# Filter spectra and forward transform in three products of split parts, and modulation pieces of 128 columns, in a two-layer Hyena and attention block

## Chip, cores and metric

The kernel runs on one core of a Trainium2 chip. The metric is the device time of one execution in microseconds (us); lower is better. The time before is 1493.73 us, the median of 3 runs (1493.24 to 1494.67). Differences of about 0.2% (3 us) are what a measurement of this kernel can tell from none.

## The reference, cut to what matters

Layer 0 is a bidirectional Hyena mixer over 512 latent tokens and, with the same weights, over 256 context tokens; layer 1 is grouped-query attention. In front of each layer stands a modulation of the normalised tokens, and behind it a gate, both from a condition vector (one for latents, one for context):

```
sh, sc, gt = jnp.split(sc_lat @ ada_w[i] + ada_b[i], 3, axis=-1)      # ada_w[i]: 1024 x 3072
h_lat = rms_norm(x_lat, norm_g[i]) * (1.0 + sc[:, None]) + sh[:, None]
...
proj = h @ w_in                                                       # 1024 -> 4 * 2048
x0, x1, v = jnp.split(short_conv(proj[..., :3 * E_HY], conv_w, conv_b), 3, axis=-1)
u = x1 * v
k = hyena_filter(L, ...)                                              # from a small MLP, per channel
U = jnp.fft.rfft(u, n=2 * L, axis=1); K = jnp.fft.rfft(k, n=2 * L, axis=0)
y = jnp.fft.irfft(U * K[None], n=2 * L, axis=1)[:, :L]
y = ((y + u * d_skip) * x0) * silu(z)                                 # then @ w_out
```

All in float32. The change touches the computation of K from k, of U from u, and of the modulation rows `sc_lat @ ada_w + ada_b`.

## The kernel before

Matrix products that need float32 accuracy are made in one of two ways. A float32 matmul is given to TensorE as it is, which the trace shows as two matmul records for one. A product in split parts (`mm3`, L69 to L72) first splits each operand into a high part, rounded to 12 bits (type fp32r), and the rest; three fp32r matmuls (high by high, high by low, low by high) then add up in one PSUM tile. The high part of a tile is a cast on ScalarE, the low part a subtraction, for the weights mostly on GpSimd (`load_w`, L121 and L122: `stg` is the loaded tile, `whi` and `wlo` are its parts, two buffers of each).

Layer 0 runs in eight rounds g = 0 to 7, each for 256 of the 2048 channels, that is two tiles of 128 (j = 0, 1). A round has eight in-projections of 128 rows: `x1` and `v` of tile a, `x1` and `v` of tile b (both in `u_stage`), `z` of a (`z_stage`), `x0` of a (`x0_stage`), `z` of b, `x0` of b. One in-projection is eight steps (`in_step`, L453) of six fp32r matmuls, three of 512 columns for latents (tiles plx, plv, plz) and three of 256 for context (pcx, pcv, pcz). Between two steps is a slot, in which another piece of work can be issued to PE. The order within an engine is the order in which the program emits its instructions; a hand-written table `steps` (L673) and a list for each in-projection say what goes into which slot:

- `kdft(g, set)` (L408): spectra of the filter for four sets m, p, 0 (letters o/O) and c. The small letter emits the sums F = a + b and F = a - b on GpSimd (L424 and L425, tile `F`); the capital letter emits the matmuls `ks` with the constant `kmat` (L436: two PSUM tiles of 512 columns, each two matmuls of 256 columns), ScalarE's copy `ko` (L439), and VectorE's two sums `kt` (L442).
- `knorm` (n, N), `y_stage` of the round before (y, Y; matmuls `pq`, L603).
- a: one entry of the list `todo`, the modulation. Before, a piece has 256 columns of `ada_w` (tile `adw`, 1 MB by one DMA) and makes two entries. The first, `ada_rows` (L174 to L182), is 8 float32 matmuls `adar` of 256 columns that use 32 columns of the array each, in four groups that run side by side, and ScalarE's copy `adr`. The second, `ada_end` (L184), turns the sum over the four groups into columns by two matmuls `adap` (L189), or, for the pieces that belong to a gate, into rows by one matmul of 256 columns (L197), with a DMA of the bias in front and one or two DMAs to `g_scr` behind. There are 16 pieces. In rounds 1 to 7 the table has two letters a among `u_stage` and the `z` of tile a, and the `x0` of tile b carries two more, one behind its second step and one behind its last.
- `spectra(g, jt)` (L562): in the `x0` of tile a (jt = 0) and the `z` of tile b (jt = 1), three calls of `fwd` (L535: matmuls `pu`, two of 256 columns with `kfwd` as the stationary operand and `ut` moving), and VectorE's products with the filter spectra: `times` (L547), the sums (L571) and `combine` (L556, L557).
- The `x0` of tile b carries nothing of `spectra`, but the six lag tiles `pk` of the next round's filter (two matmuls each, L375 and L376, and VectorE's multiplication by the decay `dec`, L378, which comes by DMA into two buffers).

`ut`, the transposed u, is made by PE transposes (`turned`, L526 to L531) and one copy of ScalarE. All of ks, pu, pk, pq, pn, ut, adar and adap take their PSUM tile from one pool of four buffers in turn (`axt`): a matmul that takes a buffer waits until its reader of four tiles before is done.

Of the kernel before, what the change touches and what calls it, by code (L numbers as in the profile page):

```python
# [11 lines left out]
F32 = mybir.dt.float32  # L12
F32R = mybir.dt.float32r
# [6 lines left out]
P = 128  # L20
# [32 lines left out]
def hybrid_kernel(ctx: ExitStack, tc: tile.TileContext, x, c, ctxt, c_ctx, norm_g, ada_w, ada_b,  # L53
                  hy_w_in, hy_conv_w, hy_conv_b, fw1, fb1, fw2, fb2, fw3, fb3, fw4, freq, hy_d,
                  hy_w_out, at_w_in, at_q_g, at_k_g, at_w_out,
                  k_f, k_i, k_k, k_z, k_dec, k_rope, out, dbg=None):
# [25 lines left out]
    ones = gp.tile([P, P], F32, tag="ones", name="ones")  # L82
# [85 lines left out]
    def ada_load(l, o0):  # L168

        t = hp.tile([P, KD, 256], F32, tag="adw", name=f"adw_{l}_{o0}")  # L170
        nc.sync.dma_start(t, ada_w[l][:, o0:o0 + 256].rearrange("(k p) o -> p k o", p=P))
        return t

    def ada_rows(t, nm):  # L174

        pt = axt(f"adar{nm}")
        for k in range(KD):
            q = k % 4 * 32
            TE.matmul(pt[q:q + 32, 0:256], silp[:, k, :], t[:, k, :], start=k < 4, stop=k >= 4)
        r = hp.tile([P, 256], F32, tag="adr", name=f"adr{nm}")  # L180
        S.copy(r, pt[:, 0:256])
        return r  # L182

    def ada_end(l, o0, r, nm):  # L184

        pt = axt(f"adap{nm}")
        if o0 < 2 * DM:
            for j in range(2):
                TE.matmul(pt[:, 2 * j:2 * j + 2], r[:, j * P:(j + 1) * P], sel, start=True, stop=True)  # L189
            c_ = o0 // P  # L190
            V.tensor_tensor(ada[l].rearrange("p (s c) -> p c s", s=2)[:, c_:c_ + 2, :],
                            pt[:, 0:4].rearrange("p (j s) -> p j s", j=2),
                            vb[:, 32 + l * 24 + c_:32 + l * 24 + c_ + 2].unsqueeze(2).broadcast_to([P, 2, 2]), ALU.add)
# [1114 lines left out]
```

## Time and profile before

| | us |
|---|---|
| median of 3 runs | 1493.73 |
| the profiled execution | 1493.93 |
| its span, first to last instruction | 1492.1 |
| TensorE (PE) busy | 1465.7 (98%) |
| VectorE (DVE) busy | 1070.2 (72%) |
| ScalarE (ACT) busy | 516.8 (35%) |
| GpSimd (POOL) busy | 408.5 (27%) |

The granted clock of TensorE is 0.997 of full speed over the span. The rounds of layer 0 stand between about 50 and 812 us of the trace; a round takes some 95 us. A matmul's busy time overlaps that of its neighbours; what a group of matmuls takes of PE is read from the starts of the matmuls around it. Rows of the timeline give the start, the duration, the engine, the line, the operation, output and inputs, the shape, how many instructions were drawn together, and in brackets the idle time in front and what ended it.

### The profile page before, as it was taken

Reading aid. Unit: us, or ns where it says so; the run is one execution under the profiler, and the core shown is the slowest. Engines: PE = TensorE matmul, PEld = TensorE weight load, DVE = VectorE, ACT = ScalarE, POOL = GpSimd, SP = SyncE. Lnnn points to the kernel's source line nnn. Section 1 sums busy time; section 2 is a strip of 40 time slices with the busy share of each in tenths; the row PEclk is TensorE's granted clock in tenths of the full one; section 3 lists DMA queues with packets and bytes.
Section 4 is the critical chain, followed back from the end, with each engine's and each line's share of the span. In section 5 each row is a group of like instructions: output and inputs, shape, how many; then the busy total and the mean of one; then the engine's idle time right before and its main releaser. Section 6 shows DMA issues by size and latency. Waiting matters only on the chain. (4 is left out here: it accounts for less than half of the span.)

```text
span 1492.1 us, 22543 instructions
## 1 busy us (share of the span) xinstructions
PE 1465.7 (98%) x8791; PEld 1255.9 (84%) x8791; DVE 1070.2 (72%) x1864; ACT 516.8 (35%) x1009; POOL 408.5 (27%) x384
## 2 busy tenths in 40 slices
PE   8999999999999999999999999999999999999998
PEld 1788887888878888888888878799998998998987
DVE  5768759578495784966849454656787878878886
ACT  3432221222213222122132243534445444445442
POOL 3431523325234243342444351211110000000005
PEclk9999999999999999999999999999999999999999
DMA  8622323323233133231322776255222312312111
GB/s 297 190 86 78 97 59 92 99 81 89 78 92 93 54 109 92 71 113 50 96 93 85 280 253 198 74 155 173 93 92 72 99 43 71 98 44 71 57 62 66
DMA packets 158402, 156.66 MB, mean 105 GB/s; under 512 B 6683, under 2 KB 138354, under 8 KB 157784
## 3 DMA queue, kind: packets, MB, share of 16 engines
q1 hardware_dynamic: 154296, 134.77, 29.0%
q0 software_dynamic: 3856, 19.93, 3.8%
q8 instruction: 69, 1.13, 0.3%
q10 hardware_dynamic: 144, 0.52, 0.1%
q14 instruction: 37, 0.30, 0.1%
HBM read 137.36 MB, written 17.84 MB: 104 GB/s over the span
## 5 line engine op out<-in xcount | busy, mean ns | idle before, releaser
L122 POOL TENSOR_TENSOR wlo<-stg,whi 128x1024 fp32r<-128x1024 f32 x64 | 159.2, 2488 | 331.9 <-ACT whi L121 331.9
L121 ACT CAST whi<-stg 128x1024 fp32r<-128x1024 f32 x99 | 103.9, 1049 | 320.1 <-issue 135.2
L873 POOL TENSOR_TENSOR r2q<-s2q,mhalf 128x2 f32<-128x2 f32 x32 | 23.4, 731 | 343.6 <-DVE s2q L871 343.6
L455 PE MATMUL plx<-h_hi,whi 128*128 128x512 f32 x248 | 107.5, 433 | 0.0
L1102 ACT ACTIVATE E<-sc,st 128x768 f32<-128x768 f32 x64 | 57.7, 902 | 126.8 <-DVE st L1100 114.0
L459 PE MATMUL plx<-h_hi,wlo 128*128 128x512 f32 x248 | 98.0, 395 | 0.0
L456 PE MATMUL plx<-h_lo,whi 128*128 128x512 f32 x248 | 97.5, 393 | 0.0
L1099 DVE TENSOR_REDUCE st<-sc 128x1 f32<-128x768 f32 x64 | 61.0, 953 | 17.5 <-PE sc L72 17.2
L460 PE MATMUL pcx<-hc_hi,wlo 128*128 128x256 f32 x248 | 69.5, 280 | 0.0
L457 PE MATMUL pcx<-hc_hi,whi 128*128 128x256 f32 x248 | 69.5, 280 | 0.0
L458 PE MATMUL pcx<-hc_lo,whi 128*128 128x256 f32 x248 | 69.4, 280 | 0.0
L1119 DVE TENSOR_TENSOR ptl<-et,pth 128x768 fp32r<-128x768 f32 x64 | 61.1, 954 | 5.3 <-ACT pth L1118 4.0
L752 DVE TENSOR_TENSOR yl<-yf,yh 128x768 fp32r<-128x768 f32 x26 | 26.0, 1002 | 52.2 <-ACT yh L751 46.9
L1118 ACT CAST pth<-et 128x768 fp32r<-128x768 f32 x64 | 51.1, 799 | 31.2 <-PE et L1114 31.0
L455 PEld LDWEIGHTS plx<-h_hi,whi 128*128 128x128 f32 x248 | 46.7, 188 | 16.3 <-issue 7.5
L455 PE MATMUL plz<-h_hi,whi 128*128 128x512 f32 x128 | 58.0, 453 | 0.0
L457 PEld LDWEIGHTS pcx<-hc_hi,whi 128*128 128x128 f32 x248 | 46.5, 188 | 11.1
L458 PEld LDWEIGHTS pcx<-hc_lo,whi 128*128 128x128 f32 x248 | 46.5, 187 | 10.8
L72 PE MATMUL po<-pth,kvt 128*128 128x256 f32 x192 | 54.1, 282 | 0.0
L71 PE MATMUL po<-ptl,kvt 128*128 128x256 f32 x192 | 54.0, 281 | 0.0
L70 PE MATMUL po<-pth,kvt 128*128 128x256 f32 x192 | 53.9, 281 | 0.0
L611 ACT ACTIVATE qs<-pq,rn 128x256 f32<-128x256 f32 (+1 forms) x32 | 13.5, 420 | 116.3 <-PE pq L603 60.6
(751 smaller groups left out, 4873.4 us busy)
## 6 DMA issues: line engine op xcount, KB each, us to landing
stg<-in_hy_w_in_dram SPq DMA_DIRECT2D x64, 512.0 KB
stg<-in_at_w_in_dram SPq DMA_DIRECT2D x40, 512.0 KB
adw<-in_ada_w_dram SPq DMA_DIRECT2D x16, 1024.0 KB
yf<-y_scr POOLq DMA_DIRECT2D x32, 384.0 KB, 5.4
ad<-in_ada_w_dram SPq DMA_DIRECT2D x16, 512.0 KB
stg<-in_hy_w_out_dram SPq DMA_DIRECT2D x16, 512.0 KB
stg<-in_at_w_out_dram SPq DMA_DIRECT2D x16, 512.0 KB
dec<-in_k_dec_dram SPq DMA_DIRECT2D x48, 128.0 KB
```

The source lines that it names most:

```text
L72: TE.matmul(ps, ll, rh, start=False, stop=last)
L121: S.copy(hi, st)
L122: (lo_eng or lo_default[0]).tensor_tensor(lo, st, f(hi), ALU.subtract)
L455: TE.matmul(pl, hi[:, k, :], h_hi[:, k, :], start=fi, stop=False)
L456: TE.matmul(pl, hi[:, k, :], h_lo[:, k, :], start=False, stop=False)
L457: TE.matmul(pc[:, 0:LC], hi[:, k, :], hc_hi[:, k, :], start=fi, stop=False)
L458: TE.matmul(pc[:, 0:LC], hi[:, k, :], hc_lo[:, k, :], start=False, stop=False)
L459: TE.matmul(pl, lo[:, k, :], h_hi[:, k, :], start=False, stop=la)
L460: TE.matmul(pc[:, 0:LC], lo[:, k, :], hc_hi[:, k, :], start=False, stop=la)
L1099: V.tensor_reduce(st[:, 0:1], sc[:, 0:T], AX.X, ALU.max)
L1102: S.activation(E, sc[:, 0:T], AF.Exp, bias=st[:, 1:2], scale=scale, accum_out=st[:, 2:3])
L1119: V.tensor_tensor(pts[n // 2][1][:, :, o:o + P], tv, f(dh), ALU.subtract)
```

## The change

1. `kdft` and `fwd` use `mm3`. The constants come from the host as high and low parts (`k_khi`, `k_klo`, `k_fhi`, `k_flo`: four DMAs on GpSimd's queue rather than two). Behind each F stand a cast `Fh` on ScalarE and a subtraction `Fl` on GpSimd; F itself now has 1 buffer rather than 4, `Fh` and `Fl` have 2 each. `ut` becomes `uth` (ScalarE's copy) and `utl` (VectorE, PSUM tile minus `uth`), 1 buffer each rather than 2.
2. The modulation pieces have 128 columns: 32 pieces, 512 KB each. One entry of `todo` (`item`) now issues the 8 matmuls `adar` of a piece and the one matmul `adap` of the piece before. All pieces are summed to columns (L187, 128x2) with VectorE's bias sum (L188). The gate's rows are made once behind the last round: `gate_rows`, three PE transposes, one copy and three DMAs.
3. The first row of the table for rounds 1 to 7 gets one more a, in the `x1` of tile a behind the sixth step.

```diff
-        pt = axt(f"adap{nm}")
-        if o0 < 2 * DM:
-            for j in range(2):
-                TE.matmul(pt[:, 2 * j:2 * j + 2], r[:, j * P:(j + 1) * P], sel, start=True, stop=True)
...
-        TE.matmul(pt[0:2, 0:256], sel, r, start=True, stop=True)
...
+        pt, c_ = axt(f"adap{nm}"), o0 // P
+        TE.matmul(pt[:, 0:2], r, sel, start=True, stop=True)
+        V.tensor_scalar(ada[l].rearrange("p (s c) -> p c s", s=2)[:, c_, :], pt[:, 0:2],
+                        vb[:, 32 + l * 24 + c_:32 + l * 24 + c_ + 1], None, ALU.add)
...
-            F = kg.tile([P, 512], F32, tag="F", name=f"F{g}{nm}{par}", bufs=4)
+            F = kg.tile([P, 512], F32, tag="F", name=f"F{g}{nm}{par}")
...
-            banks.append(F)
+            Fh = kg.tile([P, 512], F32R, tag="Fh", name=f"Fh{g}{nm}{par}", bufs=2)
+            Fl = kg.tile([P, 512], F32R, tag="Fl", name=f"Fl{g}{nm}{par}", bufs=2)
+            S.copy(Fh, F)
+            G.tensor_tensor(Fl, F, f(Fh), ALU.subtract)
+            banks.append((Fh, Fl))
...
-                    TE.matmul(pt[:, r_], kmat[:, mset, par, cs, :], banks[par][:, r_], start=True, stop=True)
+                    Fh, Fl = banks[par]
+                    mm3(pt[:, r_], kmat[0][:, mset, par, cs, :], kmat[1][:, mset, par, cs, :],
+                        Fh[:, r_], Fl[:, r_], True, True)
...
-            S.copy(ut[:, b:b + n, j * P:(j + 1) * P], pv)
+            dh = uth[:, b:b + n, j * P:(j + 1) * P]
+            S.copy(dh, pv)
+            V.tensor_tensor(utl[:, b:b + n, j * P:(j + 1) * P], pv, f(dh), ALU.subtract)
...
-            TE.matmul(pu[:, cs * 256:(cs + 1) * 256], kfwd[:, cs, c_], ut[:, 2 * b + cs, :], start=True, stop=True)
+            mm3(pu[:, cs * 256:(cs + 1) * 256], kfwd[0][:, cs, c_], kfwd[1][:, cs, c_],
+                uth[:, 2 * b + cs, :], utl[:, 2 * b + cs, :], True, True)
...
-        for n in range(len(pieces)):
-            todo.extend([lambda n=n: products(n), lambda n=n: end(n)])
+        def item(n):
+            if n < len(pieces):
+                l, o0 = pieces[n]
+                r = ada_rows(adw.pop(0), f"_{l}_{o0}")
+            if n:
+                ada_end(*pieces[n - 1], box.pop(), f"_{pieces[n - 1][0]}_{pieces[n - 1][1]}")
...
-    steps = (("m - y - - - - -", "- - Mp - Y - - -", "- - Po - - a - -", "- n Oc - N - - -", "- - C - a - - -"),
+    steps = (("m - y - - a - -", "- - Mp - Y - - -", "- - Po - - a - -", "- n Oc - N - - -", "- - C - a - - -"),
```

What this moves on the engines is shown at three places. A row gives the line, the operation, output and inputs, the shape, and in brackets the semaphores that it waits for.

First, PE at the second slot of the `x0` of tile b in round 1 (plx0_3, pcx0_3 are its PSUM tiles). Before, the slot holds the eight products `adar` alone:

```order
L459 MATMUL plx0_3_1985<-h_hi_69,wlo16_1981 128x512
L460 MATMUL pcx0_3_1986<-hc_hi_71,wlo16_1981 128x256
L179 MATMUL adar_0_2816_1999<-adw_0_2816_1579,silp_128 32x256 [waits DMAHW6_49,PE_49]
L179 MATMUL adar_0_2816_1999<-adw_0_2816_1579,silp_128 32x256 x7
L455 MATMUL plx0_3_1985<-h_hi_69,whi16_1980 128x512
L456 MATMUL plx0_3_1985<-h_lo_70,whi16_1980 128x512
```

Now it is followed by the sum of the piece before, which waits for VectorE:

```order
L465 MATMUL plx0_3_2224<-h_hi_69,wlo16_2220 128x512
L466 MATMUL pcx0_3_2225<-hc_hi_71,wlo16_2220 128x256
L179 MATMUL adar_0_2944_2238<-adw_0_2944_1970,silp_128 32x128 [waits DMAHW7_49,PE_49]
L179 MATMUL adar_0_2944_2238<-adw_0_2944_1970,silp_128 32x128 x7
L187 MATMUL adap_0_2816_2249<-sel_131,adr_0_2816_1965 128x2 [waits DVE_49,PE_49]
L461 MATMUL plx0_3_2224<-h_hi_69,whi16_2219 128x512
L462 MATMUL plx0_3_2224<-h_lo_70,whi16_2219 128x512
```

The products became half as wide, and a second PSUM tile is taken in this slot: `adap` needs the buffer of the transform pu of (g, b = 0, jt = 1), which VectorE reads in its product ab·11a (· stands for the round).

Second, PE at the end of the same in-projection. Before, the last lag tile `pk2_5` is followed by the sum of the piece whose products stood in the second slot:

```order
L460 MATMUL pcx0_3_1986<-hc_hi_71,wlo16_1981 128x256
L375 MATMUL pk2_5_2091<-w4h2_2021,h3_199 128x512 [waits DVE_49]
L376 MATMUL pk2_5_2091<-w4l2_2022,h3_199 128x512
L197 MATMUL adap_0_2816_2095<-adr_0_2816_2008,sel_131 2x256 [waits DVE_49]
L455 MATMUL plx1_4_2116<-h_hi_69,whi17_2111 128x512
L456 MATMUL plx1_4_2116<-h_lo_70,whi17_2111 128x512
```

Now a whole item stands there:

```order
L466 MATMUL pcx0_3_2225<-hc_hi_71,wlo16_2220 128x256
L375 MATMUL pk2_5_2333<-w4h2_2263,h3_199 128x512 [waits DVE_49]
L376 MATMUL pk2_5_2333<-w4l2_2264,h3_199 128x512
L179 MATMUL adar_1_0_2337<-adw_1_0_2252,silp_128 32x128 [waits DMAHW3_49,DVE_49]
L179 MATMUL adar_1_0_2337<-adw_1_0_2252,silp_128 32x128 x7
L187 MATMUL adap_0_2944_2348<-sel_131,adr_0_2944_2247 128x2 [waits DVE_49]
L461 MATMUL plx1_4_2367<-h_hi_69,whi17_2362 128x512
```

It waits for VectorE's multiplications of two lag tiles, `pk2_2` (the products) and `pk2_3` (the sum), where one wait for `pk2_2` stood.

Third, POOL at the start of round 3 (F3m0 and F3m1 are the two tiles F of set m, wlo26 the low part of a weight tile). Before:

```order
L424 TENSOR_TENSOR F3m0_2930<-kfl3_2834 128x256 [waits DVE_49]
L425 TENSOR_TENSOR F3m0_2930<-kfl3_2834 128x256
L424 TENSOR_TENSOR F3m1_2933<-kfl3_2834 128x256
L425 TENSOR_TENSOR F3m1_2933<-kfl3_2834 128x256
L424 TENSOR_TENSOR F3p0_3049<-kfl3_2834 128x256
L425 TENSOR_TENSOR F3p0_3049<-kfl3_2834 128x256
L122 TENSOR_TENSOR wlo26_3013<-stg26_3011,whi26_3012 128x1024 [waits DMAHW5_49,PE_49,Activation_49]
```

Now:

```order
L424 TENSOR_TENSOR F3m0_3320<-kfl3_3212 128x256 [waits DVE_49]
L425 TENSOR_TENSOR F3m0_3320<-kfl3_3212 128x256
L122 TENSOR_TENSOR wlo26_3427<-stg26_3425,whi26_3426 128x1024 [waits DMAHW7_49,PE_49,Activation_49]
L431 TENSOR_TENSOR Fl3m0_3324<-F3m0_3320,Fh3m0_3323 128x512 [waits Activation_49]
L424 TENSOR_TENSOR F3m1_3327<-kfl3_3212 128x256 [waits DVE_49,Pool_49]
L425 TENSOR_TENSOR F3m1_3327<-kfl3_3212 128x256
L431 TENSOR_TENSOR Fl3m1_3331<-F3m1_3327,Fh3m1_3330 128x512 [waits Activation_49]
```

Each F is followed by its `Fl`, which waits for ScalarE's cast `Fh`; the second F waits for the first `Fl`, since F has one buffer, and `wlo26` moved ahead of the first `Fl`.

## Rows read from the trace of the kernel before

**Rows 1.** Busy time by stretch: us, then busy (x count) of each engine, clock.

```profile
296.80:308.20 11.40, 11.40 (x68) 10.14 (x67) 4.09 (x7) 3.68 (x7) 3.70 (x2) 1.00 0.27 77
319.50:330.70 11.20, 11.20 (x74) 9.15 (x73) 11.17 (x15) 2.19 (x4) 2.38 (x1) 1.00 0.18 52
```

**Rows 2.** Timeline of PE: a plain step's border, and one forward transform.

```profile
320.32 0.28 PE L460 MATMUL pcz<-hc_hi,wlo 128*128 128x256 f32 x1
...
320.67 0.39 PE L456 MATMUL plz<-h_lo,whi 128*128 128x512 f32 x1
...
321.37 0.28 PE L460 MATMUL pcz<-hc_hi,wlo 128*128 128x256 f32 x1
321.49 1.02 PE L541 MATMUL pu<-ut,kfwd 128*128 128x256 f32 x4
...
322.58 0.40 PE L456 MATMUL plz<-h_lo,whi 128*128 128x512 f32 x1
```

**Rows 3.** Timeline of PE: one set of filter spectra (round 3, set m).

```profile
354.47 0.28 PE L460 MATMUL pcv<-hc_hi,wlo 128*128 128x256 f32 x1
354.59 1.89 PE L436 MATMUL ks3m<-F3m,kmat 128*128 128x256 f32 x8
...
356.55 0.39 PE L456 MATMUL plv<-h_lo,whi 128*128 128x512 f32 x1
```

**Rows 4.** Timeline of PE: products of a piece, round 2, second slot of x0 b.

```profile
327.49 0.28 PE L460 MATMUL pcx<-hc_hi,wlo 128*128 128x256 f32 x1
327.70 1.07 PE L179 MATMUL adar<-adw,silp 128*32 128x256 f32 x16
...
329.04 0.39 PE L456 MATMUL plx<-h_lo,whi 128*128 128x512 f32 x1
```

**Rows 5.** Timeline of PE: sum of a gate piece behind the last round.

```profile
811.70 0.28 PE L460 MATMUL pcx<-hc_hi,wlo 128*128 128x256 f32 x1
811.91 0.59 PE L197 MATMUL adap<-adr,sel 128*2 128x256 f32 x2
...
812.77 0.39 PE L71 MATMUL po<-wlo,yhl 128*128 128x512 f32 x1
```

**Rows 6.** Timeline of DVE: products of round 2, and a lag multiplication behind.

```profile
308.62 1.23 DVE L547 TENSOR_TENSOR ab200b<-pu,kt2m 128x1024 f32<-128x1024 f32 x1 [0.68 <-PE pu L541]
...
326.61 2.58 DVE L556 TENSOR_TENSOR Y<-ab210a 128x256 f32<-128x256 f32 x1
329.11 0.41 DVE L557 TENSOR_TENSOR Y<-ab210a 128x256 f32<-128x256 f32 x1
329.44 1.21 DVE L547 TENSOR_TENSOR ab211a<-pu,kt2p 128x1024 f32<-128x1024 f32 x1
...
339.01 1.29 DVE L378 TENSOR_TENSOR kfl<-pk,dec 128x512 f32<-128x512 f32 x2 [2.04 <-DMA dec<-in_k_dec_dram]
```

**Rows 7.** Timeline of PE: waits in the x0 of tile b, round 2.

```profile
331.93 0.47 PE L375 MATMUL pk<-w4h,h 128*128 128x512 f32 x1 [0.38 <-DVE ab211b L547]
...
339.76 0.61 PE L189 MATMUL adap<-sel,adr 128*128 128x2 f32 x4 [0.98 <-DVE kfl L378]
340.23 0.49 PE L455 MATMUL plx<-h_hi,whi 128*128 128x512 f32 x1
```

**Rows 8.** Timeline of DVE: last operation of the last convolution, round 7.

```profile
815.18 0.47 DVE L505 SCALAR_TENSOR_TENSOR cvx<-pcx,vb,cvx 128x255 f32<-128x255 f32 x1
```

**Rows 9.** Timeline of POOL and of ACT, rounds 2 and 3.

```profile
340.64 0.74 POOL L424 TENSOR_TENSOR F3m<-kfl 128x256 f32<-128x256 f32 x1 [11.74 <-DVE kfl L382]
...
355.96 1.46 POOL L424 TENSOR_TENSOR F<-kfl 128x256 f32<-128x256 f32 x1
...
394.57 1.31 POOL L365 TENSOR_TENSOR w4l<-w4s,w4h 128x512 fp32r<-128x512 f32 x1 [4.51 <-ACT w4h L364]
...
393.88 0.62 ACT L364 CAST w4h<-w4s 128x512 fp32r<-128x512 f32 x1 [4.41 <-DMA w4s<-in_hy_fw_dram]
```

**Rows 10.** Chain that ended last, out-projection: start us, us, what.

```profile
884.54 3.79 POOL xr L771 x3
```

More of the change, by code (lines that the diff above doesn't have):

```diff
@@ L81, in hybrid_kernel @@
     make_identity(nc, ident)
-    ones = gp.tile([P, P], F32, tag="ones", name="ones")
+    ones = gp.tile([P, 1], F32, tag="ones", name="ones")
     G.memset(ones, 1.0)
@@ L300, in hybrid_kernel @@
     halves = [ytile(f"x{i}") for i in range(6)]
-    ux = [hp.tile([P, 6, 256], F32, tag="ut", name=f"xut{i}", bufs=2) for i in range(2)]
+    ux = [f(hp.tile([P, 6, 256], F32R, tag=t, name=f"x{t}")) for t in ("uth", "utl")]
     halves += [u_[:, 2 * i:2 * i + 2, :].rearrange("p a b -> p (a b)") for u_ in ux for i in range(3)]
@@ L522, in u_stage @@
         if j == 0:
-            uts[g] = hp.tile([P, 6, 256], F32, tag="ut", name=f"ut{g}", bufs=2)
-        ut = uts[g]
+            uts[g] = [hp.tile([P, 6, 256], F32R, tag=t, name=f"{t}{g}") for t in ("uth", "utl")]
+        uth, utl = uts[g]
         def turned(b, n):
@@ L623, in ada_items @@
         box = []
-        def products(n):
-            l, o0 = pieces[n]
-            if n == 0:
-                adw.append(ada_load(l, o0))
-            box.append(ada_rows(adw.pop(0), f"_{l}_{o0}"))
+        def item(n):
[4 more added lines that the diff above has]
+                ada_end(*pieces[n - 1], box.pop(), f"_{pieces[n - 1][0]}_{pieces[n - 1][1]}")
+            if n < len(pieces):
+                box.append(r)
             if n + 1 < len(pieces):
                 adw.append(ada_load(*pieces[n + 1]))
-        def end(n):
-            l, o0 = pieces[n]
-            ada_end(l, o0, box.pop(0), f"_{l}_{o0}")
-        for n in range(len(pieces)):
-            todo.extend([lambda n=n: products(n), lambda n=n: end(n)])
-    ada_items([(l, o) for l, a, b in ((0, 2048, 3072), (1, 0, 3072)) for o in range(a, b, 256)])
+        for n in range(len(pieces) + 1):
+            todo.append(lambda n=n: item(n))
+    pieces = [(l, o) for l, a, b in ((0, 2048, 3072), (1, 0, 3072)) for o in range(a, b, P)]
+    ada_items(pieces)
     def ada_next():
@@ L661, in hybrid_kernel @@
     begin((16, 32), filter_items(0))
[L662 to L665 removed]
+    adw.append(ada_load(*pieces[0]))
+    kmat = []
+    for i, src in enumerate((k_khi, k_klo)):
+        kmat.append(k0.tile([P, 2, 2, 2, P], F32R, tag=f"kmat{i}", name=f"kmat{i}"))
+        with after(hc_done[2]):
+            G.dma_start(kmat[i], src.rearrange("p (a b c d) -> p a b c d", a=2, b=2, c=2))
     kinv = kg.tile([P, 2, 2, P], F32, tag="kinv", name="kinv")
     nc.sync.dma_start(kinv, k_i.rearrange("p (a b c) -> p a b c", a=2, b=2))
[L668 to L669 removed]
+    kfwd = []
+    for i, src in enumerate((k_fhi, k_flo)):
+        t = k0.tile([P, 2, 256], F32R, tag=f"kfwd{i}", name=f"kfwd{i}")
+        with after(hc_done[2]):
+            G.dma_start(t, src.rearrange("p (a b) -> p a b", a=2))
+        kfwd.append(t)
     none = lambda: None
[L673 removed]
+    steps = (("m - y - - a - -", "- - Mp - Y - - -", "- - Po - - a - -", "- n Oc - N - - -", "- - C - a - - -"),
              ("- - - - - - - -", "- - - - - - - -", "nm - - - Mp - - -", "N Po - - - Oc - -", "- a - C - a - -"))
@@ L700, in hybrid_kernel @@
     make_gsc(1)
+    gate_rows()
     p0.close()
@@ L733, in early_tiles @@
             return yf, t[:, 0, 0:T], t[:, 1, 0:T]
-        t = hp.tile([P, 6, 256], F32R, tag="ut", name=f"yhl{cht}", bufs=2)
+        t = hp.tile([P, 6, 256], F32R, tag=("uth", "utl")[cht - 1], name=f"yhl{cht}")
         return yf, *(t[:, 3 * i:3 * i + 3, :].rearrange("p a b -> p (a b)") for i in range(2))
```

56 lines of the change are left out of this document (28 added, 28 removed).

## The prediction, made before the changed kernel was run

> **What bounds the kernel now.** I read the page's busy times first: PE 98%, everything else below 75%, granted clock 0.997. So a microsecond taken off PE is worth a microsecond, unless PE then waits. Where it would wait is in the windows: in round 2 DVE is 4.09 of 11.40 us busy just ahead of the products, and 11.17 of 11.20 us during them [rows 1]. The timeline says why: from ab200b, the last product that still waits for PE (0.68 us), VectorE runs through its products without a gap until it waits for a lag's decay [rows 6], and PE waits for it twice in the `x0` of tile b, 0.38 us ahead of a lag tile and 0.98 us ahead of the last sum [rows 7]. Each round thus has two kinds of stretch: `u_stage` and the `z` of tile a, paced by PE; and the rest, in which DVE is as long as PE.
>
> **The change part by part.** The price of a group on PE is the time from the start of the six-matmul step's last matmul ahead of it to the start of the second one behind, less that of a plain border, 320.67 - 320.32 = 0.35 us [rows 2].
>
> Filter spectra: 356.55 - 354.47 - 0.35 = 1.73 us for eight records, 0.216 each [rows 3]; now 12 fp32r matmuls of 256 columns. One of these takes 321.49 - 321.37 = 0.12 us [rows 2] (and one of 512 columns the other 0.23 of the border), so 1.42 us, 0.31 less. Four sets in 8 rounds: 32 x 0.31 = 9.9 us, or 1.23 a round, all in the stretch that PE paces. Forward transforms: 322.58 - 321.37 - 0.35 = 0.86 us [rows 2]; now 6 x 0.12 = 0.71, 0.15 less; six a round, 48 in all, 7.2 us, or 0.9 a round, all in the stretch that DVE fills.
>
> Here a rule speaks: the Trainium skill, "TensorE: Matmul & The Clock Gate", section "Back-to-back issue gap", gives 262 cycles (109 ns) for an isolated matmul of 256 columns and 131 ns a matmul of 512 for a sustained stream. The trace sides with neither (0.12 and 0.23 us). An estimate by its 109 ns makes the two savings 13.5 and 9.9 us and not 9.9 and 7.2; nothing below uses that.
>
> Modulation: the products of a piece take 329.04 - 327.49 - 0.35 = 1.20 us [rows 4], of which four rounds of 0.216 are matmuls and 0.33 entry and exit. Half as wide: 0.43 + 0.33 = 0.77 us (bounds: 0.60, half of all; 1.20, if the weight loads pace it). A sum costs 0.47 us from start to start in its four-record form [rows 7] and 812.77 - 811.70 - 0.35 = 0.72 us as a gate row [rows 5]; the new one has two short records, 0.22 us. An item is 0.99 us (0.8 to 1.4). Before: 16 x 1.20 + 8 x 0.47 + 8 x 0.72 = 28.7 us; after: 32 x 0.99 = 31.7. PE work grows by 3.0 us here, but moves forward: five items a round use the list up in round 6, where four entries lasted to the end.
>
> Sum over PE alone: -9.9 - 7.2 + 3.0 = -14.1 us. Now by stretch, since not all of it stays.
>
> (a) `u_stage` and `z` of a, rounds 1 to 6: -1.23 of spectra. Three items (2.97) take the place of one piece's products and one sum (1.67, with a gate sum 1.92): +1.30 in four rounds, +1.05 in two. Sum: 4 x 0.07 - 2 x 0.18 = -0.1 us (-4 to +3 by the item's bounds).
>
> (b) Round 0: -1.23; its two entries cost the same as before. Its sets follow closely behind the filter, so that each of the first has less cover for `Fh` and `Fl`, 0.62 + 1.31 = 1.93 us [rows 9]; 0 to 3.9 for two such, and I take half, 1.9. Sum +0.7.
>
> (c) For the other rounds the chain F, `Fh`, `Fl` must be hidden. By rows 9 a set is twice 0.74 x 2 + 0.62 + 1.31 = 3.4, that is 6.8 us, and a `wlo` of 2.38 [rows 1] is now in between: 9.2 us. F of set m starts at 340.64, its matmuls at 354.59 [rows 3, 9]: 4.7 us to spare. That hides it; without cover each us late would be one on PE. `utl`, two short passes a tile on DVE, and `Fh` on ACT fall where DVE is a third busy [rows 1].
>
> (d) Products and `x0` of b, rounds 0 to 5. The second slot now has a sum that needs the buffer of ab·11a. In round 2 that is free at 329.44 + 1.21 = 330.65 [rows 6]. The transforms bring it forward: two stand ahead of ab200b (0.3 us), all six ahead of the `wlo` that prolongs an operation of the chain, 2.58 against 0.41 us [rows 6]; I take 0.7 of 0.3 to 1.1, so 329.95. PE comes there at 327.70 - 0.9 + 0.77 = 327.6: a new wait of 2.4 us. From then on PE has work without a pause: 0.22 for the sum, 0.34 to the second matmul of the next step [rows 4], then what lay between 329.04 and 339.76 less its two waits [rows 4, 7], 9.36, then 0.77 for the products: the last sum starts at 340.64, 0.88 later than before, and is 0.25 shorter. So +0.6 us a round (0 to +1.0), +3.6 in six rounds: the transforms' 0.9 and the old waits' 1.36 are gone into the new wait and 0.8 of modulation.
>
> (e) `x0` of b in round 6 has only one sum left. Lag tile 1 waits for ab611b as before, 0.3 us earlier; from there PE runs as before, without the last sum (0.72) and its wait (0.98): -2.0 us (-0.9 to -3).
>
> (f) Round 7 has no item: -1.23, and -1.20 - 0.72 in the PE-paced stretch: -3.1 us. Its `x0` of b loses 1.92 more, but the out-projection's fifth tile needs the convolution, done at 815.18 + 0.47 [rows 8] at the end of the same DVE chain; that chain loses the gate's sum ahead of it and starts 0.3 earlier. I keep -0.7 (0 to -1.9). The gate's three transposes stand in that wait.
>
> Sum: -0.1 + 0.7 + 3.6 - 2.0 - 3.1 - 0.7 = -1.6 us. The profiled execution, 1493.9, is 0.2 above the median. So 1493.9 - 1.6 - 0.2 = **1492.1 us**, own range 1488 to 1496.
>
> **The rivals.** *PE keeps it.* If the `wlo` no longer falls on one of the two operations of the chain that read SBUF twice (2.58 against 0.41 [rows 6]), ab·11a is 2.2 us earlier, the new wait is nearly gone, and (d) turns from +0.6 to about -1.2 a round: 1492.1 - 6 x 1.8 = 1481; half of the rounds or of the effect gives 1486. For it: POOL's starts follow PE's, which come forward by other amounts than DVE's. Against: `wlo` starts when PE frees the weights, DVE's chain moves the same way by half, and the operation is hit in both tiles of every round.
>
> *A late chain, the slower side.* In sets 0 and c of rounds 1 to 7, `Fh` has two buffers and must wait for the matmuls of the set before; what follows is one `Fh`, `Fl`, F, `Fh`, `Fl`: 0.62 + 1.31 + 1.48 + 0.62 + 1.31 = 5.3 us. F has been seen at twice its time, 1.46 [rows 9]; with that, and a `wlo` of 2.38 in front of it, it is 9.2 of some 11 us between two sets, which stand an in-projection (11.4 us [rows 1]) apart. It decides from 2 us more. A us of lateness in each of these 14 places is 14 us: 1506; in one set a round 7: 1499. The rows show F prolonged next to a `wlo` and not by more.
>
> A rule leans that way. The Trainium skill, "SBUF — State Buffer", section "SBUF: two separate sides", says that a VectorE operation with two SBUF inputs and a GpSimd operation that reads SBUF exclude each other for a whole instruction. The trace agrees (2.58 us for an operation of 0.41 [rows 6]). By it the 64 new `Fl` could cost DVE up to 64 x 1.31 = 84 us; they stand where DVE idles 7.3 of 11.4 us [rows 1], so it is the chain of POOL and not that of DVE which would be late.
>
> *It comes back later.* The chain that ended last runs through GpSimd's work (3.79 us of `xr` at 884 [rows 10]) between the rounds and the out-projection's second half. If that keeps its clock time, what (e) and (f) gain is lost behind it: 1492.1 + 5.8 = 1498 at worst, 1494.5 if (d) is half as dear and half of it is lost. Against: it starts behind the rounds and moves with them.
>
> **How the numbers follow.** Chances: the forecast 0.54, PE keeps it 0.22, a late chain 0.16, it comes back 0.08. A measurement can tell 0.2%, 3 us: faster is below 1490.7, slower above 1496.7. Faster: 0.22 and 0.16 of the forecast's lower end, 0.38. Same: 0.32 of the forecast and the 0.08 of the last rival, 0.40. Slower: 0.16, and 0.06 of upper ends, 0.22. The range leaves out the far half of the first rival (0.1) and the upper part of the second (0.1): 1483.5 to 1499.5.
>
> **What would show it.** Right: `ks` groups of 1.4 and `pu` groups of 0.7 us on PE; items of 1.0; in rounds 0 to 5 a wait of 2 to 3 us of the sum in the second slot for ab·11a, and the old waits gone; rounds 1 to 5 within 1 us of 95; the gain all in rounds 6 and 7. Wrong: waits of `ks` for `Fl`; `x0` of b without the wait and rounds of 94 us; an item well off 1.0; a wait of the out-projection near 889 us.

## The result, and the profile of the changed kernel

The changed kernel takes 1505.06 us (median of four runs, 1503.77 to 1505.57) against 1493.49 us before on the same chip: ratio 1.0073, 95% interval 1.0061 to 1.0085. The forecast was 1492.1 us with a range of 1483.5 to 1499.5, so it was wrong in sign and by 13 us. In the profiled executions the span grew from 1492.1 to 1502.0 us, by 9.9 us.

**The prices were right.** The matmuls cost what was forecast. These are rows of PE's timeline (start, length, instruction), one filter set of round 3 and one forward transform of round 2; they answer [rows 3] and [rows 2]:

```profile
364.60 0.28 PE L466 MATMUL pcv<-hc_hi,wlo 128*128 128x256 f32 x1
364.72 0.28 PE L70 MATMUL ks3m<-Fh3m,kmat 128*128 128x256 f32 x1
...
366.38 0.39 PE L462 MATMUL plv<-h_lo,whi 128*128 128x512 f32 x1
```

```profile
324.77 0.28 PE L466 MATMUL pcz<-hc_hi,wlo 128*128 128x256 f32 x1
...
325.83 0.39 PE L462 MATMUL plz<-h_lo,whi 128*128 128x512 f32 x1
```

By the prediction's way of reading, a set costs 366.38 - 364.60 - 0.35 = 1.43 us (forecast 1.42, before 1.73) and a transform 325.83 - 324.77 - 0.35 = 0.71 (forecast 0.71, before 0.86).

**The waits.** TensorE's waits between 60 and 900 us of the changed kernel, by what ended them (sum, times, longest). There are six of the first line, one a round in rounds 0 to 5, and one is shown; lines of 0.5 us and less are left out:

```profile
PE adap L187 <- DVE ab111a L556: 2.9, 1, 2.9
...
PE po L70 <- ACT whi L121: 2.2, 1, 2.2
PE adar L179 <- DMA adw<-in_ada_w_dram: 2.1, 1, 2.1
PE po L71 <- POOL wlo L122: 1.6, 1, 1.6
PE pk L375 <- DVE ab611a L556: 1.2, 1, 1.2
PE ks L71 <- POOL Fl L431: 1.0, 1, 1.0
PE ks0p L70 <- ACT Fh0p L430: 0.6, 1, 0.6
```

The two waits of [rows 7] in the `x0` of tile b are gone, and the sum's wait for ab·11a has come in their place, as term (d) said (2.9 us, forecast 2.4). The waits for `Fh` and `Fl` stand only in round 0, 1.6 us together (forecast 1.9). Four lines were not in the forecast: `adw` in round 0, `whi` and `wlo` at the start of the out-projection, and a lag tile's wait of 1.2 us for ab611a in round 6, where term (e) had kept the old one of 0.4.

**The clock.** The larger surprise is in a column that the forecast did not price at all. Stretches of 4 us of the changed kernel, in round 1 (around its wait for ab111a) and in round 2 (around the one for ab211a); columns are us, busy time and count of PE, PEld, DVE, ACT and POOL, then the granted TensorE clock, the DMA share and GB/s:

```profile
240.00:244.00 4.00, 2.06 (x7) 1.89 (x8) 4.00 (x6) 0.27 (x1) 0.04 (x1) 0.75 0.62 178
244.00:248.00 4.00, 4.00 (x19) 3.37 (x19) 3.45 (x8) 0.00 (x0) 0.00 (x0) 0.83 0.35 88
...
340.00:344.00 4.00, 4.00 (x24) 3.44 (x23) 3.97 (x8) 0.00 (x0) 0.00 (x0) 1.00 0.78 215
```

In round 1 the granted clock falls behind the wait, and in round 2, behind a wait of the same length, it doesn't. What that does is seen on PE's timeline, first round 2, then round 1:

```profile
335.32 0.28 PE L466 MATMUL pcx<-hc_hi,wlo 128*128 128x256 f32 x1
335.53 0.64 PE L179 MATMUL adar<-adw,silp 128*32 128x128 f32 x16
339.10 0.35 PE L187 MATMUL adap<-sel,adr 128*128 128x2 f32 x2 [2.93 <-DVE ab211a L556]
...
339.63 0.39 PE L462 MATMUL plx<-h_lo,whi 128*128 128x512 f32 x1
339.86 0.28 PE L463 MATMUL pcx<-hc_hi,whi 128*128 128x256 f32 x1
```

```profile
241.94 0.54 PE L187 MATMUL adap<-sel,adr 128*128 128x2 f32 x2 [2.93 <-DVE ab111a L556]
...
242.91 0.63 PE L462 MATMUL plx<-h_lo,whi 128*128 128x512 f32 x1
243.34 0.41 PE L463 MATMUL pcx<-hc_hi,whi 128*128 128x256 f32 x1
```

From start to start a matmul of 512 columns takes 339.86 - 339.63 = 0.23 us in round 2 and 243.34 - 242.91 = 0.43 in round 1: the lower of the two levels, 1.2 GHz, from 241.94 to about 245.3. I count what that costs as the sum of (1 - granted clock) x 4 us over the stretches of 4 us: (1 - 0.75) x 4 + (1 - 0.83) x 4 = 1.7 us in round 1. The lengths of the rounds check this count. From the first matmul of set m to the next round's,

```profile
171.98 0.28 PE L70 MATMUL ks1m<-Fh1m,kmat 128*128 128x256 f32 x1
...
269.14 0.28 PE L70 MATMUL ks2m<-Fh2m,kmat 128*128 128x256 f32 x1
```

round 1 takes 97.16 us, and round 2, with the same wait and no such stretch, 364.72 - 269.14 = 95.58; rounds 3 to 5 take 95.58 to 95.60. So the stretch costs 1.6 us of the round. The whole kernel from 60 to 1480 us has 10.2 us by the count: 1.7 in round 0 behind `adw`, 1.7 each in rounds 0 and 1 behind the sum's wait, 1.7 in round 6 behind the lag tile's shorter wait for ab611a (1.2), and 3.4 at the start of the out-projection. The kernel before has none; its waits there are 1.2 us at most. The Trainium skill, "TensorE: Matmul & The Clock Gate", section "HAM oscillation — how this bites in real kernels", describes a loop in which PE waits some 3 to 5 us for a DMA in every slice and starts every next slice at the lower clock. This trace agrees in part: with shorter waits, of 2.9 us, a stretch at the lower clock follows in rounds 0 and 1 and not in rounds 2 to 5.

**The start of the out-projection.** SyncE's own queue waits 28.0 us for the gate rows, and ScalarE and PE show what stands behind. First the queue's longest wait, then ScalarE, then PE, all of the changed kernel:

```profile
SPq L199 <- ACT gates L197: 28.0, 1, 28.0
```

```profile
816.91 0.45 ACT L197 COPY gates<-gates 8x384 f32<-8x384 f32 x1
817.27 1.04 ACT L121 CAST whi<-stg 128x1024 fp32r<-128x1024 f32 x1
```

```profile
815.70 0.49 PE L196 MATMUL gates<-ident,ada 128*8 128x128 f32 x3
818.36 0.84 PE L70 MATMUL po<-whi,yhl 128*128 128x512 f32 x2 [2.17 <-ACT whi L121]
820.79 0.80 PE L71 MATMUL po<-wlo,yhl 128*128 128x512 f32 x1 [1.59 <-POOL wlo L122]
821.38 0.63 PE L72 MATMUL po<-whi,yhl 128*128 128x512 f32 x1
821.81 0.63 PE L71 MATMUL po<-wlo,yhl 128*128 128x512 f32 x1
```

The gates' copy needs the last transposes of PE, the cast of the first output weights (`whi`) follows it on ScalarE, and PE stands idle for both and for `wlo`, and runs at half clock behind (0.43 us from 821.38 to 821.81 for 512 columns). Of the 3.4 us counted there about 0.8 falls into the wait for `wlo` itself, half of its 1.59 us, by my estimate, and costs nothing more. Before, PE had no wait there: the cast came at 802 us, ahead of the last convolution.

**Where the 9.9 us are.** The table takes the start of set m's matmuls in each round on PE (in round 3, 364.72 against 354.59 [rows 3]) and the end of the last product of round 7 on DVE, subtracts the kernel before, and takes differences. "Repaired" is the last kernel of the experiments, c2_b4_filler_early_piece.

| stretch | forecast | changed kernel | repaired |
|---|---|---|---|
| round 0 | +0.7 + 0.6 = +1.3 | +7.9 | +2.5 |
| rounds 1 to 5 | -0.1 + 5 x 0.6 = +2.9 | +2.8 | +2.4 |
| round 6 | -2.0 | -1.7 | -2.8 |
| round 7 to its last product | -3.1 | -4.5 | -4.0 |
| from there to the end | -0.7 | +5.4 | -1.6 |
| sum of the spans | -1.6 | +9.9 | -3.4 |

The miss is in two places, round 0 (6.6 us) and the start of the out-projection (6.1 us).

### The profile page after: what moved, and what is told of

The parts are those of the page before. It is cut to its first block, busy times and chain, and to the rows that moved or that the text cites. A ratio compares the mean times of both kernels' runs of the same rounds, so it can differ in the third digit from the quotient of the medians.

```text
span 1502.0 us, 23828 instructions
## 1 busy us (share of the span) xinstructions
PE 1460.5 (97%) x9290; PEld 1265.8 (84%) x9290; DVE 1078.2 (72%) x1912; ACT 557.2 (37%) x1090; POOL 492.9 (33%) x450
## 5 line engine op out<-in xcount | busy, mean ns | idle before, releaser
L461 PE MATMUL plx<-h_hi,whi 128*128 128x512 f32 x248 | 102.7, 414 | 0.2 <-DVE cvx L511 0.2
L539 DVE TENSOR_TENSOR utl<-ut,uth 128x512 fp32r<-128x512 f32 (+1 forms) x32 | 16.4, 553 | 65.2 <-ACT uth L538 65.2
L461 PE MATMUL plz<-h_hi,whi 128*128 128x512 f32 x128 | 52.6, 411 | 0.0
```

Of the source, the lines that this page charges most:

```text
L461: TE.matmul(pl, hi[:, k, :], h_hi[:, k, :], start=fi, stop=False)
```

## The experiments

My theory after the first look had two parts: waits of two to three us now cost more than their length, since the clock falls behind some of them; and the gate rows, written once behind the last round, hold up the out-projection. The rival was that the changed pieces themselves cost the time (order, transfers, the longer list).

**Modulation alone.** The spectra and transforms of the kernel before, with the pieces of 128 columns, the new items and the gate rows of the change. The other half, split spectra with pieces of 256 columns (p1_spectra, expected at about 1481 us), has no time: its tiles for layer 0 need 68 kB a partition where 61.125 are left, so the two halves of the change hang together and that expectation is untested.

```diff
-            todo.extend([lambda n=n: products(n), lambda n=n: end(n)])
+            todo.append(lambda n=n: item(n))
...
+    gate_rows()
```

> Parts 2 and 3 alone: pieces of 128 columns, all to columns, one more a, gate rows at the end; spectra and transform in float32 as before. Theory (the loss is all here: a wait in the second slot of the last in-projection in six rounds, the gate rows in front of the out-projection's first weights, and drops of the clock behind these waits): 1510 to 1518 us. Rival (only the 3 us of PE work count, and the loss comes from both parts together): 1496 to 1499.

Measured: 1514.06 us, ratio 1.0123 (1.0108 to 1.0138), as the theory had it. So the split parts do pay: the whole change is 9 us faster than this half. Its profile has the six waits for ab·11a (2.4 us each), those for `whi` and `wlo` (2.2 and 1.7), and again 10.2 us of clock loss, this time in rounds 0, 1, 2, 3 and 5 and at the end. The waits come with the modulation, and which of them the clock falls behind differs from kernel to kernel.

**The gate rows later.** The call of `gate_rows` moved behind the last inverse transform of round 7.

```diff
-    gate_rows()
...
+            y_stage(7, j)
+    gate_rows()
```

> The changed kernel with gate_rows moved from in front of the out-projection to behind its third channel tile and the last inverse transforms, nothing else. Theory: the waits of the out-projection's first matmuls for whi (2.17 us) and wlo (1.59 us) go, and with them the drop of the clock behind them (about 3.4 us lost at 0.5 to 0.85): about 1498 us. Rival (the products of the last round and the convolution hold the out-projection anyway): 1503 to 1505.

Measured: 1518.13 us, ratio 1.0153 (1.0136 to 1.0170), slower still; the expectation fell. The profiled execution is the fastest of the four, 1513.17 against 1517.6 to 1518.9 for the others. PE's waits at the end are now other ones:

```profile
PE po L70 <- ACT yh L766: 5.7, 1, 5.7
PE po L70 <- DVE cvx L511: 4.3, 1, 4.3
PE po L72 <- POOL yl L767: 3.0, 1, 3.0
```

Without the gates in its way GpSimd prepares the out-projection's operands earlier, in the middle of round 7's products, and the last convolution `cvx` comes late; and the gates' writes still stand ahead of a later weight load on SyncE's queue (840.2 and 841.3 us).

**The sum moved.** The sum for a piece is taken out of the second slot of the `x0` of tile b (where it waits for ab·11a) and stands at its end and in the next `z` of tile a; the second slot has the products alone. The products that stood at the end of the `x0` of tile b move behind the last step of the `v` of tile b, in `u_stage`, so that a round still makes five pieces.

```diff
-        x0_stage(g, 1, [none, ada_next] + filter_items(g + 1) + [ada_next])
+        x0_stage(g, 1, [none, ada_products] + filter_items(g + 1) + [ada_total])
```

> The changed kernel with the sum adap taken out of the second slot of the last in-projection: it stands at the end of z of tile a, the last slot has one sum alone, and one more item stands in u_stage, so that each round still makes five pieces. Theory: the wait of 2.9 us for ab11a in six rounds goes and so do the drops of the clock behind it in rounds 0, 1 and 6 (1.7 us each): about 1499 us, PE's last in-projection again held by DVE at its lag tiles. Rival (DVE sets the end of this stretch in any order, and the clock does not matter): 1503 to 1505.

Measured: 1495.62 us, ratio 1.0007 (0.9998 to 1.0017), 9.4 us less than the changed kernel and 3.4 less than expected. The six waits and all half-clock stretches of the rounds are gone; 1.7 us of clock loss is left, at 812 us. What replaces the 2.9 us in rounds 0 to 5 are waits of the lag tiles for ab·11a and ab·1c, 0.7 us and less each. So the wait's own length was worth little: rounds 2 to 5 take 95.13 to 95.18 us in place of 95.58 to 95.60, 0.4 less, while round 1, which loses its half-clock stretch too, goes from 97.16 to 95.14, 2.0 less. The wait for `adw` in round 0 is still there, 1.7 us, and this time no stretch follows it.

**A filler.** To part the wait's length from what the clock does behind it, the order of the change is kept and PE is given 22 matmuls of 256 columns, whose results nobody reads, between the products and the sum of the second slot.

```diff
+        for _ in range(fill[0]):
+            TE.matmul(pt[:, 256:512], h_hi[:, 0, 0:P], h_hi[:, 0, 0:256], start=True, stop=True)
```

> The changed kernel with 22 matmuls of 256 columns more (about 2.6 us of PE) between the products and the sum in the second slot of the last in-projection, where PE waits 2.9 us for ab11a in rounds 0 to 5. Their results, in columns of the PSUM tile that nobody reads, are not used; the output is that of the changed kernel. Theory (a wait costs its length and the drop of the granted clock behind it): the wait shrinks to some 0.3 us, the rounds' length is otherwise unchanged, the drops behind it in rounds 0 and 1 (1.7 us each) go: about 1501.5 us. Rival (the clock does not follow from the wait, more work is only more work): 1505 to 1508.

Measured: 1498.98 us, ratio 1.0030 (1.0020 to 1.0040). Useless work makes the kernel 6 us faster than the changed one, 2.5 us more than expected: the wait's own 2.9 us remain, filled, and in the profile the half-clock stretches behind the filled waits of rounds 0 and 1 are gone (3.4 us). The one of round 6 is gone too, though its wait of 1.2 us is not filled and is still there, so that one comes or stays away by itself. The clock loss is 5.1 us, where the changed kernel has 10.2. A wait's length and the clock behind it are two prices. Not all of the 6.1 us is placed by this: in the two profiled executions rounds 0 to 5, which have the filled waits, are 1.9 us shorter together (rounds 0 and 1 by 2.8, while rounds 2 to 5 are 0.2 us longer each), and the rest of their difference of 5.6 lies in round 6 and outside the rounds.

**The gate rows earlier.** `gate_rows` moved into the first free slot of round 7, in the buffer of a piece (a7_gates_early). The same with the sum moved is a second kernel (a5_both), and that with the first piece of round 0 three steps earlier a third (a6_both_early_piece).

```diff
-        st = wp.tile([P, 1024], F32, tag="stg", name="gates", bufs=NST)
+        st = hp.tile([P, KD, P], F32, tag="adw", name="gates").rearrange("p k o -> p (k o)")
...
-            table = {"n": kn[0], "N": kn[1], "a": ada_next, "-": none, "y": lambda: [y() for y in ya],
+            table = {"n": kn[0], "N": kn[1], "a": ada_next if g < 7 else gates_once, "-": none, "y": lambda: [y() for y in ya],
...
-    gate_rows()
```

> The changed kernel with gate_rows in round 7, in the sixth slot of its first in-projection, where all columns have been there for a round, with its rows in the tile adw in place of a weight buffer; nothing else. Theory (gate_rows in front of the out-projection holds ScalarE's cast of the first weights, SP's queue of weight loads and one of three weight buffers): the waits of 2.2 and 1.6 us and 3.4 us of lowered clock behind them go, less up to 4.3 us if the earlier preparation on POOL prolongs the products' chain of round 7: 1498 to 1502 us. Rival (the out-projection starts late for another reason): 1505.

> The sum moved out of the second slot and gate_rows in round 7, together. Theory: 1495.6 less the waits of 3.9 us for whi and wlo and 1.7 us of lowered clock behind them: 1490; if POOL's earlier preparation prolongs the products of round 7 by 4 us: 1494. Rival (nothing is left to gain): 1495.6.

```diff
-             ("- - - - - - - -", "- - - - - - - -", "nm - - - Mp - - -", "N Po - - - Oc - -", "- a - C - a - s"))
+             ("- - - - - - - -", "- - - - - - - -", "nm - - - Mp - - -", "N Po - - - Oc - a", "- - - C - a - s"))
```

> As the kernel with both, and the first piece of round 0 stands three steps earlier (behind the last step of v of tile b, in place of the second slot of z of tile a), so that the load of the second piece has about 8 us in place of 4.6. Theory: the wait for adw (1.7 to 2.1 us) goes, the rest stays: 1.7 to 2 us below the kernel with both. Rival (another wait takes its place in round 0): no difference.

Measured: 1509.53 us (ratio 1.0098, 1.0075 to 1.0121) for the gates alone, 1498.58 (1.0028, 1.0015 to 1.0042) with the sum moved, 1495.88 (1.0008, 0.9998 to 1.0019) with the earlier piece too. The early piece held: the wait for `adw` in round 0 is gone with the clock loss behind it, 2.7 us. The early gates failed twice: 4.5 us slower on the changed kernel and 3.0 slower on the moved sum. The waits for `whi` and `wlo` did go, but a longer one came, here of the third kernel:

```profile
PE po L70 <- DVE cvx L511: 6.6, 1, 6.6
```

Why, the timelines of GpSimd and of VectorE in that kernel show, around 801 us:

```profile
800.36 3.38 POOL L122 TENSOR_TENSOR wlx<-stg,whx 128x1024 fp32r<-128x1024 f32 x1
803.70 2.58 POOL L122 TENSOR_TENSOR wlo<-stg,whi 128x1024 fp32r<-128x1024 f32 x1
```

```profile
798.61 2.88 DVE L580 TENSOR_TENSOR ab710a<-ab710a,ab710b 128x1024 f32<-128x1024 f32 x1
801.52 2.50 DVE L565 TENSOR_TENSOR Y<-ab710a 128x256 f32<-128x256 f32 x1
803.94 2.62 DVE L566 TENSOR_TENSOR Y<-ab710a 128x256 f32<-128x256 f32 x1
806.49 1.21 DVE L556 TENSOR_TENSOR ab711a<-pu,kt7p 128x1024 f32<-128x1024 f32 x1
```

The two operations of L565 and L566 (L556 and L557 of the kernel before) take 0.4 us with no subtraction of GpSimd beside them [rows 6]; beside a GpSimd subtraction they take 2.5 and 2.6. The product of L556, which reads one operand from PSUM, keeps its 1.21. (L580's 2.88 stands beside an earlier subtraction of GpSimd.)

**The preparation held back.** So the weights and the row that GpSimd prepares too early were given the two buffers of the products themselves, which come free only behind the last products of round 7. This was run on the third kernel (b3_late_lows) and, with the sum left where the change put it, on the kernel with the early gates alone (b4_gates_early_late_lows).

```diff
+              abtile(f"yf0_{cht}")[:, 0:T] if cht == 2 else
...
+                                         st=abtile("stgab") if (half, cht) == (0, 2) else None)
```

> The kernel of a6_both_early_piece, with the weight piece 66 and the row yf0_2 of the out-projection put into the two product tiles (ab) instead of tiles that come free earlier. So their loads can't start before the last products of round 7 are read, and POOL's subtractions for them (wlx66 3.38 us at 800.36 and one of the two yhl of 4.42 us together at 795.99 in a6) move behind the chain of sums. Theory (POOL's subtractions, freed early by the missing hold of the gates, stretch VectorE's two-input operations): L565 2.50 at 801.52 and L566 2.62 at 803.94 fall back to 0.42 each, L565 2.45 at 810.12 may stay; the wait of TensorE for cvx L511, 6.6 us, falls by 4.3 to 6; no half-clock stretch behind it (3.4 us of clock loss in a6, some 1.7 to 3 of it there). Sum: 1495.9 - 4 to - 6, so 1490 to 1492. Rival (the wait for cvx is the chain's own length, or what is moved back comes late for the out-projection's second and third step instead): 1494.5 to 1497.

> The kernel of a7_gates_early (the changed kernel with its gate rows in round 7's first slot, 1509.5) with the same two tiles as in b3_late_lows; the sum of slot 2 stays where the change put it. Theory: the same stretch is taken out of round 7, so the 6.6 us wait for cvx falls by 4 to 6: 1503.5 to 1505.5, about the changed kernel itself or a little under, with the six waits for ab11a of 2.9 us and their half-clock stretches in rounds 0 and 1 unchanged. Rival (the stretch in a7 was the chain's own lateness of 2.9 us that the moved sum carries into round 7): 1508 to 1511.

Measured: 1490.37 us on the third kernel, ratio 0.9975 (0.9965 to 0.9985), and 1501.92 us on the other, ratio 1.0047 (1.0032 to 1.0063). The theory held in the first; the second came 1.6 us below its range, for a reason that the next run looks for. The wait for the convolution is now 0.5 us in both kernels; VectorE in the faster one, where L566 is back at 0.41 and one stretched operation, beside a `wlo` that is needed there, remains:

```profile
800.95 2.51 DVE L565 TENSOR_TENSOR Y<-ab710a 128x256 f32<-128x256 f32 x1
803.38 0.41 DVE L566 TENSOR_TENSOR Y<-ab710a 128x256 f32<-128x256 f32 x1
```

The runs of the other kernel fall into two groups, three at 1495.2 to 1496.2 us with a mean granted clock of 0.995 to 0.996, and seven at 1500.8 to 1504.4 with 0.991 to 0.992. Its profiled execution is one of the first group. It has all six waits of 2.9 us for ab·11a, and the clock behind the one of round 1 is whole:

```profile
240.00:244.00 4.00, 3.23 (x18) 2.88 (x19) 3.97 (x7) 0.27 (x1) 0.00 (x0) 1.00 0.93 258
```

The seven others, without a profile each, have the lower mean clock alone to show for their 5 to 9 us: 0.004 of 1500 us is 6 us. That a longer stretch at half clock can stand behind one such wait is seen in a7_gates_early, in round 1 behind its wait of 2.92 us:

```profile
240.00:244.00 4.00, 1.08 (x15) 0.84 (x8) 4.00 (x4) 0.17 (x1) 1.34 (x1) 0.85 0.28 70
244.00:248.00 4.00, 4.00 (x13) 3.39 (x13) 3.38 (x6) 0.09 (x1) 0.00 (x0) 0.50 0.70 192
248.00:252.00 4.00, 4.00 (x18) 3.30 (x17) 2.00 (x5) 0.00 (x0) 0.00 (x0) 0.80 0.15 43
```

That is 3.4 us by the count, twice that of the changed kernel, and the round takes 98.50 us, 2.9 more than one without a stretch.

**The filler again.** If the two groups differ by the clock behind the six waits, PE kept busy there must bring all runs to the lower group. The last two kernels add the filler to the one with two groups, and then the earlier first piece.

```diff
-        x0_stage(g, 1, [none, ada_next] + filter_items(g + 1) + [ada_next])
+        x0_stage(g, 1, [none, ada_filled] + filter_items(g + 1) + [ada_next])
```

> The kernel of b4_gates_early_late_lows with the 22 dummy matmuls of a3_filler in the second slot of the x0 of tile b (they compute nothing that is read). b4's ten runs lie at 1495.2 to 1496.2 and at 1500.8 to 1504.4; its profiled one, 1495.2, has the six waits of 2.9 us for ab11a and only one stretch of half clock (1.7 us, behind the wait for adw in round 0). Theory (the upper runs have half-clock stretches behind the six waits, 1.7 us each in some of the rounds): with TensorE busy in the slot these can't come, so all runs lie near the lower group: median 1495 to 1497, range under 3 us. Rival (the upper runs come from elsewhere, a transfer or the end): median 1500 to 1503 and a range of 8 us as before.

> c1_b4_filler with the first piece of round 0 three steps earlier, as in a6_both_early_piece. Theory: the wait of 1.8 us for adw in round 0 and the half-clock stretch behind it (1.7 us) go: 3.5 us under c1, 1491.5 to 1493.5. Rival (the piece's load only moves the wait to another step): as c1, 1495 to 1497.

Measured: 1496.14 us, ratio 1.0010 (1.0001 to 1.0019), and 1492.75 us, ratio 0.9989 (0.9980 to 0.9999). Nine of the first one's ten runs lie between 1494.6 and 1497.3 us at a clock of 0.997 or 0.998, and the tenth, 1500.07, has 0.994: the range was to be under 3 us and is 5.5 with that run. The median held, and the step between the two, 3.4 us, was forecast as 3.5, though not as the sum that was forecast: the first one's profiled execution has the wait for `adw`, 2.0 us, and no half-clock stretch behind it or anywhere in the rounds, so the second term of the 3.5 is not shown. The profile of the first (c1_b4_filler) in round 1: the filler and the sum on PE's timeline, and the clock around the sum:

```profile
237.74 2.89 PE L183 MATMUL adar<-h_hi 128*128 128x256 f32 x22
240.75 0.35 PE L191 MATMUL adap<-sel,adr 128*128 128x2 f32 x2
```

```profile
240.00:244.00 4.00, 3.88 (x24) 3.32 (x23) 3.93 (x6) 0.27 (x1) 0.00 (x0) 1.00 0.95 263
```

## Why the prediction was wrong, point by point

- **The reading of the bound and the prices** held: a set 1.43 us (1.42), a transform 0.71 (0.71); an item in round 2, from 335.32 (start of the last matmul ahead of it) to 339.63, is 4.31 - 0.35 - 2.93 = 1.03 us (0.99).
- **(a) and (d), rounds 1 to 5**: +2.8 us measured, +2.9 forecast, and that is luck, since 1.6 of the +2.8 is the clock in round 1, which was not in the sum; the rest is +1.2. The mechanism of (d) is in the trace, the six waits. They are 2.9 us and not 2.4 mostly because the step "I take 0.7" was mis-sized. The first transform of round 2 on PE before, the same now, and VectorE's product now:

```profile
305.65 1.02 PE L541 MATMUL pu<-ut,kfwd 128*128 128x256 f32 x4
```

```profile
314.34 0.28 PE L70 MATMUL pu<-uth,kfwd 128*128 128x256 f32 x1
```

```profile
337.75 1.21 DVE L556 TENSOR_TENSOR ab211a<-pu,kt2p 128x1024 f32<-128x1024 f32 x1
```

  The transforms begin 314.34 - 305.65 = 8.69 us later than before, and ab211a, which ends at 338.96, 337.75 - 329.44 = 8.31 later [rows 6]. So the split transforms bring it forward by 0.4 us and not by 0.7.
- **(b), round 0**, failed: +7.9 us for +1.3. Its waits for `Fh` and `Fl` were 1.6 us for a forecast of 1.9. "its two entries cost the same as before" was the wrong step: round 0 now waits 2.1 us for the second piece's load, and its two waits of over two us have a half-clock stretch behind them, 3.4 us. With the first piece three steps earlier and PE kept busy, round 0 costs +2.5; the 1.2 us of that over the forecast are not explained here.
- **No price for the clock** is the step that is missing in (b), (d) and (f). A new wait of 2.4 us was put into the sum by its length alone. The filler runs show the second price: 6.1 us between the changed kernel and the one with the filler, and 5.8 us between the same two with the repaired out-projection, although in both the sum comes no earlier. The prediction read the granted clock in [rows 1], found 1.00, and did not ask whether that would stay with waits that the kernel before doesn't have.
- **(e), round 6**, -1.7 us for -2.0, with a half-clock stretch in it, behind a lag tile that waits 1.2 us for ab611a and not "as before"; without the stretch, -2.8.
- **(f), round 7**, was right in kind up to its last product, -4.5 for -3.1 us, and wrong behind it: +5.4 for -0.7. "The gate's three transposes stand in that wait" looked at PE alone. What was overlooked is that one late copy now stands ahead of the output weights on ScalarE, and three writes that wait for it 28.0 us ahead of their loads on SyncE's queue, where before each gate piece wrote its own. It costs waits of 2.2 and 1.6 us and 3.4 us of clock.
- **The rivals.** "PE keeps it" needed the `wlo` to miss VectorE's chain; it still hits (L565 takes 2.48 us at 335.01). "A late chain" names the time that came, 1499 to 1506, by a mechanism that did not: no set waits for `Fl` behind round 0. "It comes back later" was the nearest in kind, a loss behind the rounds, but at the first weights of the out-projection and not at `xr`. Its 1494.5 does not come out of its own terms: (d) half as dear and half of 5.8 lost give 1492.1 - 1.8 + 2.9 = 1493.2.
- **What the change is worth** without these two losses is close to the forecast: c2_b4_filler_early_piece, in which the pieces, the items and their order in the second slot are the change's own, is 1.3 us faster than the kernel before by its medians (1492.75 against 1494.08), for a forecast of -1.6. The sum agrees better than its parts, which miss in both directions in the table. Its profiled execution is its fastest, so the table's -3.4 flatters it by some 2 us. With the sum moved instead (b3_late_lows) it is 3.0 us faster than before, 1490.37 against 1493.41, and 14.7 us faster than the change as it stood. Neither the filler, the moved sum nor the preparation held back was tried in the kernel before, which has no such waits; what they would be worth there is not known.

**What stays open.** Which of the waits the clock falls behind. In the changed kernel it was those of rounds 0, 1 and 6, in the half with modulation alone rounds 0 to 3 and 5, with the gates early rounds 0, 1, 2 and 6, in the profile of the kernel with two groups none of them, with waits of 2.4 to 2.9 us each (1.2 in round 6). The wait for `adw` in round 0, 1.7 to 2.1 us, has a stretch behind it in five kernels and none in three (a1_gates_later, a2_sum_moved, c1_b4_filler). The runs show that keeping PE busy takes the loss away in all profiled executions, and not what decides it; the one run of c1_b4_filler at 1500.07 us has no profile.

## What to carry to other kernels

A new wait on TensorE, where it bounds the kernel, has two prices, its length and the clock behind it, and the second can be as large as the first. Of the 2.9 us of length only 0.4 a round came back when the sum was moved, since PE then waited for VectorE elsewhere. Here the waits were of 1.2 to 2.9 us, and the loss of clock behind a single one was nothing, 1.7 us or 3.4 us: for each new wait of that size, carry such a loss in the range as an upper bound. Moving work away from such a wait (9.4 us here), or filling it (6.1 us), can be worth more than the change was forecast to gain (1.6 us). And where writes that were spread out are gathered into one late copy, follow every queue that it then stands in, and ask what the buffers that it no longer holds will let start early.

## What the runs showed of the hardware that was not expected

- Behind some waits of TensorE, of 1.7 to 2.9 us and in round 6 of 1.2, the granted clock was at the lower level for a stretch: in round 1 of the changed kernel from 241.94 to about 245.3, 1.7 us by the count, and in round 1 of a7_gates_early 3.4 us. Behind others of the same length, in the same kernel, it was not. 22 useless matmuls in the wait made the kernel 6.1 us faster.
- A VectorE operation with two SBUF inputs can be held by several GpSimd operations in a row. In b3_late_lows the multiplication of L601, which takes 0.96 us in the same place of a6_both_early_piece, lasted 6.09 us beside three of them; first VectorE, then GpSimd, then PE:

```profile
812.17 6.09 DVE L601 TENSOR_TENSOR cvx<-cvx,sz 128x768 f32<-128x768 f32 x1
```

```profile
810.91 2.40 POOL L122 TENSOR_TENSOR wlo<-stg,whi 128x1024 fp32r<-128x1024 f32 x1
813.27 2.37 POOL L122 TENSOR_TENSOR wlx<-stgab,whx 128x1024 fp32r<-128x1024 f32 x1
815.59 1.85 POOL L778 TENSOR_TENSOR yhl<-yf,yhl 128x768 fp32r<-128x768 f32 x1
```

```profile
820.33 2.92 PE L612 MATMUL pq<-kinv,Y 128*128 128x128 f32 x24 [0.84 <-DVE y L622]
```

  It cost PE a wait of 0.84 us, for VectorE's next work behind the multiplication (L622); in c2_b4_filler_early_piece, where the same multiplication takes 1.95 us, that wait is not there. The Trainium skill, "SBUF — State Buffer", section "SBUF: two separate sides", has the rule: the two exclude each other for a whole instruction. The trace agrees, and adds that with GpSimd's instructions queued back to back VectorE can fail to get in between: the multiplication ends at 818.2, behind the third. It is not always so: in the rows of a6_both_early_piece above L580 ends at 801.49, L565 at 804.02 and L566 at 806.56, between and behind GpSimd's subtractions, which stand back to back too. What makes the difference is not shown.
